# RWKV scan on TensorE: readout and update in one tiling mode, a block-diagonal inverse, alternating heads in the Gram, and two runs moved into others

## The chip, the cores and the metric

The kernel runs on one core of one Trainium2 chip. The metric is the device time of one execution in microseconds (us), lower is better. The engines are TensorE (PE in the profile; its weight loads are PEld), VectorE (DVE), ScalarE (ACT), GpSimd (POOL) and SyncE (SP), which issues nearly all DMAs. Each engine works through its own instructions in order.

## The reference, cut to what matters

One layer with two groups of heads: 16 heads of forgetting attention ("fox", head dimension 128) and 32 RWKV-7 heads (dimension 64), behind one wide input projection and ahead of one output projection. Everything is float32; the sequence has 256 frames, the model 4096 columns.

```
proj = x @ w_in                      # fox q|k|v|f, rwkv r|k|v|w_down|a_down, gate z
...
state = state * w_t + (state @ a_t) b_t^T + v_t k_t^T     # per head, per frame
y_t   = state @ r_t
...
out = concat(fox, rwkv) * silu(z) @ w_out
x   = LayerNorm(ALPHA * x + out)
```

The kernel computes the recurrence of `state` in chunks of 64 frames: within a chunk the frames are coupled by a strictly triangular 64x64 matrix per head, whose inverse (with the unit diagonal) has to be applied once per chunk, and the state is carried from chunk to chunk.

## The kernel before, in words

**The main stream.** The work goes in 16 groups `i`; a group is two RWKV heads (64 rows each, so together the 128 partitions) and one fox head. For each group eight projections of 128 columns are computed (r, k, v, fox q, k, v, and two gates). Float32 weights and inputs are split into a high and a low fp32r part. `proj` (L198) loads a weight tile of 128x1024 by DMA on SyncE (L204, four buffers), ScalarE makes its high part (L135), VectorE its low part by a subtraction (L136; three buffers each), and `mm` (L139) issues for each of 32 k-blocks a pair of matmuls: the high part against 512 columns (L140) and the low part against 256 (L141). A projection is four such tiles of eight pairs.

**Slots.** After every fourth pair `slot()` (L191) advances each of a list of Python generators by one `yield`, and what they emit falls between two pairs of the main stream in TensorE's order. So a group has 64 slots, two per weight tile: one at the tile's end and one at its middle. `wait(n)` lets n slots pass; the waits of the stages are in the table `W` (L38). The framework then places tiles in buffers, adds the waits, and orders the instructions of each engine; an instruction of another engine can come earlier than its place in the code when its inputs are there. (The product of bonus and v, L451, stands after the inverse in the code and runs beside the Gram.)

**`rwkv(i)` (L364), in order:**

1. Inputs: k, the normalisation, `lt[j]` and `BK`, which hold the decayed left and right factors of the two heads `j`; `HALF[j]` are the rows of head `j`.
2. The Gram run (L406): 4 chunks for head 0, then 4 chunks for head 1, each a product of 64 rows with 128 stationary and 128 streamed columns into the PSUM tile `gp[j]`. VectorE masks one half of the result into `gb` (L415) and the other into the free half of `lt[j]` (L424). Right behind it four transposes of BK (L427).
3. The triangular blocks of 32x32 go through DRAM into another layout: `nd` (L419), `Nb` (L421). VectorE computes the inverse of all blocks row by row (L438, L439), and the result returns through `td` (L443) and four loads `T` (L446).
4. A run of v against the centring matrix (`vp`, L457), copied by ScalarE to the upper or lower halves of `SV[j]` and `UV[j]` (L462, L463).
5. `X`: four transposes of T on VectorE (L469), then two runs of 32x32 products, `qt` (L474) and `xp` (L484), that fill the off-diagonal blocks; the result of xp is copied into X for head 0 by ScalarE and for head 1 by VectorE (L487).
6. The scan over the 4 chunks c, a slot after each step: the residual `rh` (L494) and its copy R (L496); the update `up`, X times R for each head (L501), copied into `UV` (L502, L503); the new state `sp` (L508; not in the last chunk) and, in the same run, the readout `yp`: for each head one product of SV with lt (L521, 128 rows) and one of UV with gb (L522, the head's 64 rows).
7. Group norm and the gate (L525 to L543).

`fox(i)` (L545) loads `nb` (the cumulated gate of the keys, L548), and computes logits, softmax (L565 to L569), transposes of the probabilities (L573, copied to `pT`, L574) and the output (L578, copied to `o`, L580).

**Tilings.** A matmul uses the 128x128 array as a whole or a part of its rows and columns. The profile prints rows*columns of the stationary operand: 128*128 for the main stream, 64*128 for the Gram, 128*64 for rh, sp and L521, 64*64 for vp, up and L522, 32*32 for qt and xp. A float32 product appears as two matmul instructions, so the Gram of a group is x16 and rh of a chunk x4.

## Time and profile before

| | us |
|---|---|
| three runs | 2138.33, 2138.70, 2142.48 (median 2138.7) |
| the profiled execution, first to last instruction (span) | 2139.2 |
| the same less the median of the runs | 0.5 |
| TensorE busy, share of the span | 98% |
| VectorE, ScalarE | 69%, 48% |
| input projections and scan, from 70 to 1759 us: TensorE, VectorE, ScalarE busy | 1668.9, 1211.4, 827.9 of 1689.0 |
| TensorE clock granted, mean | 0.994 |

The page of the profile gives no other time of the profiled execution than its span. Rows of the timeline have the start, the duration, the engine, the line, the operation, the tiles written and read, the shape and how many instructions of the kind follow each other (x4). Matmuls are pipelined and their durations overlap, so starts say more than durations. In rows of groups the number before the comma is the busy time in all, then the mean in ns, then the idle time of the engine before such instructions and what ended it. In rows of waits the numbers are the total, the times and the longest. In rows of windows each engine has its busy time and, in brackets, the matmuls or loads in flight.

### The profile page before, as it was taken

Reading aid. Unit: us, or ns where it says so; the run is one execution under the profiler, and the core shown is the slowest. Engines: PE = TensorE matmul, PEld = TensorE weight load, DVE = VectorE, ACT = ScalarE, POOL = GpSimd, SP = SyncE. Lnnn points to the kernel's source line nnn. Section 1 sums busy time; section 2 is a strip of 40 time slices with the busy share of each in tenths; the row PEclk is TensorE's granted clock in tenths of the full one; section 3 lists DMA queues with packets and bytes.
Section 4 is the critical chain, followed back from the end, with each engine's and each line's share of the span. In section 5 each row is a group of like instructions: output and inputs, shape, how many; then the busy total and the mean of one; then the engine's idle time right before and its main releaser. Section 6 shows DMA issues by size and latency. Waiting matters only on the chain.

```text
span 2139.2 us, 33113 instructions
## 1 busy us (share of the span) xinstructions
PE 2103.2 (98%) x12558; PEld 1745.4 (82%) x12558; DVE 1478.6 (69%) x2919; ACT 1020.9 (48%) x1607; POOL 29.4 (1%) x136
## 2 busy tenths in 40 slices
PE   9999999999999999999999999999999999999997
PEld 7878887878888888887888888888888877888885
DVE  6867676767676777776676767676767686655555
ACT  6545454545454545454545454444444454433332
POOL 0000000000000000000000000000000000000000
PEclk9999999999999999999999999999999999999998
DMA  7545555545555555555555555555555555866664
GB/s 279 183 145 174 161 172 160 167 162 161 171 163 166 167 165 167 168 164 169 156 172 159 175 159 176 159 172 162 167 162 169 154 175 188 276 196 190 194 195 150
DMA packets 130865, 372.73 MB, mean 174 GB/s; under 512 B 31161, under 2 KB 40041, under 8 KB 130705
## 3 DMA queue, kind: packets, MB, share of 16 engines
q1 hardware_dynamic: 130704, 370.62, 55.3%
q8 instruction: 98, 1.61, 0.3%
q14 instruction: 63, 0.51, 0.1%
HBM read 364.23 MB, written 6.32 MB: 173 GB/s over the span
## 4 chain that ended last, share of the span: by engine, by line
PE 75%; DVE 16%; DMA 6%; issue 2%; ACT 1%; SPq 1%; DVEq 0%; ACTq 0%
PE acc L140 33%; PE acc L141 16%; PE oacc L661 6%; PE oacc L663 5%; PE oacc L662 5%; DVE xc L439 3%; DVE prod L438 3%; DVE w_1l L136 2%; DMA td<-xc 2%; DVE w_2l L136 2%; PE yp L522 2%; DMA T<-td 1%; DVE w_0l L136 1%; DMA w<-in_w_main_dram 1%; PE gp L406 1%
## 5 line engine op out<-in xcount | busy, mean ns | idle before, releaser
L140 PE MATMUL acc<-x,w_1h 128*128 128x512 f32 x1016 | 374.9, 406 | 0.4 <-ACT w_1h L135 0.4
L140 PE MATMUL acc<-x,w_2h 128*128 128x512 f32 x1016 | 374.8, 405 | 0.0
L140 PE MATMUL acc<-x,w_3h 128*128 128x512 f32 x1016 | 374.3, 405 | 0.0
L140 PE MATMUL acc<-x,w_0h 128*128 128x512 f32 x1016 | 371.3, 404 | 0.0
L141 PE MATMUL acc<-x,w_1l 128*128 128x256 f32 x1016 | 288.7, 284 | 14.2 <-DVE w_1l L136 14.2
L141 PE MATMUL acc<-x,w_2l 128*128 128x256 f32 x1016 | 285.5, 281 | 0.0
L141 PE MATMUL acc<-x,w_3l 128*128 128x256 f32 x1016 | 284.9, 280 | 0.0
L141 PE MATMUL acc<-x,w_0l 128*128 128x256 f32 x1016 | 284.9, 280 | 0.0
L140 PEld LDWEIGHTS acc<-x,w_3h 128*128 128x128 f32 x1016 | 190.6, 188 | 47.8
L140 PEld LDWEIGHTS acc<-x,w_0h 128*128 128x128 f32 x1016 | 190.7, 188 | 47.5
L140 PEld LDWEIGHTS acc<-x,w_1h 128*128 128x128 f32 x1016 | 191.5, 189 | 46.2 <-ACT w_1h L135 0.7
L140 PEld LDWEIGHTS acc<-x,w_2h 128*128 128x128 f32 x1016 | 191.2, 188 | 43.4
L135 ACT CAST w_2h<-w 128x1024 fp32r<-128x1024 f32 x127 | 133.3, 1050 | 179.4 <-PE acc L140 117.7
L141 PEld LDWEIGHTS acc<-x,w_1l 128*128 128x128 f32 x1016 | 192.6, 190 | 23.1 <-DVE w_1l L136 23.0
L135 ACT CAST w_1h<-w 128x1024 fp32r<-128x1024 f32 x127 | 132.9, 1046 | 151.6 <-PE acc L140 150.1
L135 ACT CAST w_0h<-w 128x1024 fp32r<-128x1024 f32 x127 | 133.1, 1048 | 138.4 <-PE acc L140 102.9
L136 DVE TENSOR_TENSOR w_1l<-w,w_1h 128x1024 fp32r<-128x1024 f32 x127 | 154.3, 1215 | 62.6 <-ACT w_1h L135 62.1
L141 PEld LDWEIGHTS acc<-x,w_2l 128*128 128x128 f32 x1016 | 192.5, 189 | 0.7
L141 PEld LDWEIGHTS acc<-x,w_3l 128*128 128x128 f32 x1016 | 192.0, 189 | 0.7
L141 PEld LDWEIGHTS acc<-x,w_0l 128*128 128x128 f32 x1016 | 191.9, 189 | 0.1
L136 DVE TENSOR_TENSOR w_0l<-w,w_0h 128x1024 fp32r<-128x1024 f32 x127 | 155.0, 1220 | 47.0 <-ACT w_0h L135 45.3
L136 DVE TENSOR_TENSOR w_2l<-w,w_2h 128x1024 fp32r<-128x1024 f32 x127 | 155.2, 1222 | 39.2 <-ACT w_2h L135 39.2
(690 smaller groups left out, 3305.0 us busy)
## 6 DMA issues: line engine op xcount, KB each, us to landing
w<-in_w_main_dram SPq DMA_DIRECT2D x508, 512.0 KB, 4.6
wo<-in_w_o_dram SPq DMA_DIRECT2D x128, 512.0 KB, 3.4
Nb<-nd SPq DMA_DIRECT2D x16, 512.0 KB, 6.4
res<-in_xtok_dram SPq DMA_DIRECT2D x16, 256.0 KB, 5.0
xr<-in_xt_dram SPq DMA_DIRECT2D x7, 512.0 KB
out_dram<-res SPq DMA_DIRECT2D x7, 512.0 KB, 2.7
lr<-in_w_lora_dram SPq DMA_DIRECT2D x7, 416.0 KB, 8.4
nb<-ncd SPq DMA_DIRECT2D x16, 128.0 KB, 4.4
```

What stands on the lines that cost most here:

```text
L135: nc.scalar.copy(hi[:, :n], src[:, :n])
L136: nc.vector.tensor_tensor(lo[:, :n], src[:, :n], hi[:, :n].bitcast(F32), ALU.subtract)
L140: nc.tensor.matmul(acc[:m, :], hi[:, o : o + m], xs[k].rearrange("p a t -> p (a t)"), start=(k == 0), stop=False)
L141: nc.tensor.matmul(acc[:m, :S], lo[:, o : o + m], xs[k][:, 0, :], start=False, stop=(k == KT - 1))
L406: nc.tensor.matmul(gp[j][:, c * P : (c + 1) * P], BK[h, c, :], lt[j][h, c, :], start=True, stop=True)
L438: nc.vector.tensor_tensor(prod[:, :, s + 1 :], nb[:, s : s + 1, s + 1 :].to_broadcast([P, NJ, w]), xc[:, :, s + 1 :], ALU.mult)
L439: nc.vector.tensor_reduce(xc[:, :, s : s + 1], prod[:, :, s:], AX.X, ALU.add)
L522: nc.tensor.matmul(dst, UV[j][h, c, :], gb[h, c, C:P], start=False, stop=True)
L661: nc.tensor.matmul(acc[m], ht[k][:, 0, tt], hi[:, o], start=(k == 0), stop=False)
L662: nc.tensor.matmul(acc[m], ht[k][:, 1, tt], hi[:, o], start=False, stop=False)
L663: nc.tensor.matmul(acc[m], ht[k][:, 0, tt], lo[:, o], start=False, stop=(k == KT - 1))
```

## The change

- The readout's second product takes all 128 rows: `gb` becomes two tiles that live through the whole kernel, `gb[0]` and `gb[1]`, each zero in the rows of the other head, zeroed once by GpSimd. Now sp and both readout products have the tiling 128*64. They are issued SV for head 0, SV for head 1, UV for head 0, UV for head 1.
- `X` becomes a tile of 128 columns with the two heads' inverses on its diagonal, and the update is one product of 128x128 with R instead of one per head.
- The Gram issues chunk by chunk, head 0 and head 1 in turn.
- The run `vp` moves from behind the inverse to directly behind the Gram, ahead of the transposes of BK, and takes 128 rows (`cent` is block-diagonal) instead of 64. Its copies and the product of bonus and v move with it.
- The residual of the first chunk moves into the run of `xp`; the slot between the two goes, so that the scan's later steps each come one slot sooner.
- `pT` uses the buffer of `nb`, and `o` that of `vt`.

```diff
@@ -176,8 +176,11 @@
     nc.vector.memset(gneps, GN_EPS)
     onesr = const.tile([P, P], F32R, name="onesr")
     nc.vector.tensor_copy(onesr, ones)
-    X = const.tile([P, NCH, C], F32, name="X")
+    X = const.tile([P, NCH, P], F32, name="X")
     nc.gpsimd.memset(X, 0.0)
+    gb = [const.tile([P, NCH, P], F32, name=f"gb{j}") for j in range(2)]
+    for j in range(2):
+        nc.gpsimd.memset(gb[j], 0.0)
 
     sides = []
 
@@ -400,11 +403,19 @@
         done.add(i)
         yield from wait(W["gp"])
         gp = [pst(f"gp{i}_{j}") for j in range(2)]
-        for j in range(2):
-            h = HALF[j]
-            for c in range(NCH):
+        for c in range(NCH):
+            for j in range(2):
+                h = HALF[j]
                 nc.tensor.matmul(gp[j][:, c * P : (c + 1) * P], BK[h, c, :], lt[j][h, c, :], start=True, stop=True)
-        gb = rp.tile([P, NCH, P], F32, tag="gb", name=f"gb{i}")
+        v = rk[i, 2]
+        vp = pst(f"vp{i}")
+        for c in range(NCH):
+            for j in range(2):
+                h, o = HALF[j], HALF[1 - j]
+                nc.tensor.matmul(vp[o, c * C : (c + 1) * C], v[:, c * C : (c + 1) * C], cent[:, h], start=True, stop=True)
+        tp = pst(f"tp{i}")
+        for c in range(NCH):
+            nc.tensor.transpose(tp[:, c * P : (c + 1) * P], BK[:, c, :], ident)
 
         def m(rows):
             return cs[rows, C_MASK : C_MASK + P].unsqueeze(1).to_broadcast([C, NCH, P])
@@ -412,21 +423,27 @@
         gv = [gp[j].rearrange("p (c t) -> p c t", t=P) for j in range(2)]
         for j in range(2):
             h = HALF[j]
-            nc.vector.tensor_tensor(gb[h], gv[j][h], m(h), ALU.mult)
+            nc.vector.tensor_tensor(gb[j][h], gv[j][h], m(h), ALU.mult)
...
-            nc.sync.dma_start(out=nd[q].rearrange("c r s -> r c s"), in_=gb[B * q : B * (q + 1), :, o : o + B])
+            nc.sync.dma_start(out=nd[q].rearrange("c r s -> r c s"), in_=gb[q // 2][B * q : B * (q + 1), :, o : o + B])
         nb = rp.tile([P, B, B], F32, tag="Nb", name=f"Nb{i}")
         nc.sync.dma_start(out=flat(nb), in_=nd.rearrange("q c r s -> (q c) (r s)").unsqueeze(1).to_broadcast([16, NG, B * B]))
         for j in range(2):
             o = HALF[1 - j]
             nc.vector.tensor_tensor(lt[j][o], gv[j][o], m(o), ALU.mult)
-        tp = pst(f"tp{i}")
-        for c in range(NCH):
-            nc.tensor.transpose(tp[:, c * P : (c + 1) * P], BK[:, c, :], ident)
         BKt = rp.tile([P, NCH, P], F32, tag="sbl", name=f"BKt{i}")
         nc.scalar.copy(flat(BKt), tp)
+        SV = [rp.tile([P, NCH, C], F32, tag=f"SV{j}", name=f"SV{j}_{i}") for j in range(2)]
+        UV = [rp.tile([P, NCH, C], F32, tag=f"UV{j}", name=f"UV{j}_{i}") for j in range(2)]
+        for j in range(2):
+            o = HALF[1 - j]
+            nc.scalar.copy(SV[j][o], ch(vp[:, :S])[o])
+            nc.scalar.copy(UV[j][o], ch(vp[:, :S])[o])
+            nc.gpsimd.memset(SV[j][HALF[j], 0, :], 0.0)
+        nc.vector.tensor_tensor(bon, bon, v, ALU.mult)
+        nc.scalar.activation(bon, bon, AF.Identity, bias=column("gn_bias", i))
         yield from wait(W["d1"])
         prod = rp.tile([P, NJ, B], F32, tag="prod", name=f"prod{i}")
         xc = rp.tile([P, NJ, B], F32, tag="xc", name=f"xc{i}")
@@ -444,61 +461,48 @@
         T = rp.tile([P, NCH, B], F32, tag="T", name=f"T{i}")
         for q in range(4):
             nc.sync.dma_start(out=T[B * q : B * (q + 1)], in_=td[q].rearrange("c r s -> r c s"))
-        yield from wait(4)
-        while (i, 2) not in rk:
-            yield
-        v = rk[i, 2]
-        nc.vector.tensor_tensor(bon, bon, v, ALU.mult)
-        nc.scalar.activation(bon, bon, AF.Identity, bias=column("gn_bias", i))
-        vp = pst(f"vp{i}")
-        for c in range(NCH):
-            for j in range(2):
-                h, o = HALF[j], HALF[1 - j]
-                nc.tensor.matmul(vp[o, c * C : (c + 1) * C], v[h, c * C : (c + 1) * C], cent[h, h], start=True, stop=True)
-        SV = [rp.tile([P, NCH, C], F32, tag=f"SV{j}", name=f"SV{j}_{i}") for j in range(2)]
-        UV = [rp.tile([P, NCH, C], F32, tag=f"UV{j}", name=f"UV{j}_{i}") for j in range(2)]
-        for j in range(2):
-            o = HALF[1 - j]
-            nc.scalar.copy(SV[j][o], ch(vp[:, :S])[o])
-            nc.scalar.copy(UV[j][o], ch(vp[:, :S])[o])
-            nc.gpsimd.memset(SV[j][HALF[j], 0, :], 0.0)
-        yield from wait(W["d2"] - 4)
+        yield from wait(W["d2"])
         for q in range(4):
-            o = B * (q % 2)
+            o = C * (q // 2) + B * (q % 2)
             rows = slice(B * q, B * (q + 1))
             nc.vector.transpose(X[rows, :, o : o + B], T[rows])
         qp = pst(f"qt{i}")
         for c in range(NCH):
             for j in range(2):
                 a, b = slice(C * j, C * j + B), slice(C * j + B, C * j + C)
-                nc.tensor.matmul(qp[b, c * B : (c + 1) * B], gb[a, c, B:C], T[a, c, :], start=True, stop=True)
+                nc.tensor.matmul(qp[b, c * B : (c + 1) * B], gb[j][a, c, B:C], T[a, c, :], start=True, stop=True)
         Q = rp.tile([P, NCH, B], F32, tag="Q", name=f"Q{i}")
         for j in range(2):
             b = slice(C * j + B, C * j + C)
             (nc.vector.tensor_copy if j else nc.scalar.copy)(flat(Q)[b], qp[b, :P])
+
+        def residual(c):
+            rh = pst(f"rh{i}_{c}")
+            for j in range(2):
+                nc.tensor.matmul(rh[HALF[j], :C], lt[j][:, c, 0:C], SV[j][:, c, :], start=True, stop=True)
+            R = rp.tile([P, C], F32, tag="R", name=f"R{i}_{c}", bufs=2)
+            nc.vector.tensor_copy(R, rh[:, :C])
+            return R
+
         yield from wait(W["xp"])
         xp = pst(f"xp{i}")
         for c in range(NCH):
             for j in range(2):
                 a, b = slice(C * j, C * j + B), slice(C * j + B, C * j + C)
-                nc.tensor.matmul(xp[a, c * B : (c + 1) * B], Q[b, c, :], X[b, c, B:], start=True, stop=True)
+                nc.tensor.matmul(xp[a, c * B : (c + 1) * B], Q[b, c, :], X[b, c, C * j + B : C * j + C], start=True, stop=True)
         for j in range(2):
             a = slice(C * j, C * j + B)
-            (nc.vector.tensor_copy if j else nc.scalar.copy)(X[a, :, B:], xp[a, :P].rearrange("p (c s) -> p c s", s=B))
+            (nc.vector.tensor_copy if j else nc.scalar.copy)(X[a, :, C * j + B : C * j + C], xp[a, :P].rearrange("p (c s) -> p c s", s=B))
+        R = residual(0)
         yield
 
         yp = pst(f"yp{i}")
         for c in range(NCH):
-            rh = pst(f"rh{i}_{c}")
-            for j in range(2):
-                nc.tensor.matmul(rh[HALF[j], :C], lt[j][:, c, 0:C], SV[j][:, c, :], start=True, stop=True)
-            R = rp.tile([P, C], F32, tag="R", name=f"R{i}_{c}", bufs=2)
-            nc.vector.tensor_copy(R, rh[:, :C])
-            yield
+            if c:
+                R = residual(c)
+                yield
             upp = pst(f"up{i}_{c}")
-            for j in range(2):
-                h = HALF[j]
-                nc.tensor.matmul(upp[h, :C], X[h, c, :], R[h, :], start=True, stop=True)
+            nc.tensor.matmul(upp[:, :C], X[:, c, :], R, start=True, stop=True)
             nc.vector.tensor_copy(UV[0][HALF[0], c, :], upp[HALF[0], :C])
             nc.scalar.copy(UV[1][HALF[1], c, :], upp[HALF[1], :C])
             yield
@@ -515,11 +519,9 @@
                         sl_ = rp.tile([P, C], F32, tag=f"sl{j}", name=f"sl{i}_{c}_{j}")
                         nc.scalar.mul(sl_[h], SV[j][h, c, :], lc)
                         nc.vector.scalar_tensor_tensor(SV[j][h, c + 1, :], sp[h, :C], lc, sl_[h], ALU.mult, ALU.add)
-            for j in range(2):
-                h = HALF[j]
-                dst = yp[h, c * C : (c + 1) * C]
-                nc.tensor.matmul(dst, SV[j][:, c, :], lt[j][:, c, C:P], start=True, stop=False)
-                nc.tensor.matmul(dst, UV[j][h, c, :], gb[h, c, C:P], start=False, stop=True)
+            for lhs, rhs in ((SV, lt), (UV, gb)):
+                for j in range(2):
+                    nc.tensor.matmul(yp[HALF[j], c * C : (c + 1) * C], lhs[j][:, c, :], rhs[j][:, c, C:P], start=lhs is SV, stop=lhs is UV)
             yield
 
         y2 = rt(f"y2{i}")
@@ -571,13 +573,13 @@
         pt = pst(f"fpt{i}")
         for m in range(3):
             nc.tensor.transpose(pt[:, m * P : (m + 1) * P], lg[:, m, :], ident)
-        pT = rp.tile([P, 3 * P], F32, tag="pT", name=f"pT{i}")
+        pT = rp.tile([P, 3 * P], F32, tag="nb", name=f"pT{i}")
         nc.scalar.copy(pT, pt[:, : 3 * P])
         yield from wait(W["fo"])
         op = pst(f"fop{i}")
         nc.tensor.matmul(op[:, :S], vt[:, 0, :], pT[:, :S], start=True, stop=False)
         nc.tensor.matmul(op[:, P:S], vt[:, 1, :], pT[:, S:], start=False, stop=True)
-        o = t256("fo", f"fo{i}")
+        o = t256("vt", f"fo{i}")
         nc.scalar.copy(o, op[:, :S])
         while f"f{i}" not in szs:
             yield
```

## The prediction

> **What bounds the kernel now.** I read the totals and the chain of waits first, then the matmuls of one scan in order of time, then the waits.
>
> ```profile
> PE 2103.2 (98%) x12558; PEld 1745.4 (82%) x12558; DVE 1478.6 (69%) x2919; ACT 1020.9 (48%) x1607; POOL 29.4 (1%) x136
> ...
> PE 75%; DVE 16%; DMA 6%; issue 2%; ACT 1%; SPq 1%; DVEq 0%; ACTq 0%
> ...
> L141 PE MATMUL acc<-x,w_1l 128*128 128x256 f32 x1016 | 288.7, 284 | 14.2 <-DVE w_1l L136 14.2
> ```
>
> TensorE is busy 98% of the span and is three quarters of the chain; the clearest wait inside its main stream is 14.2 us for the low halves of the weights. So time is gained by taking work or dead time out of TensorE's order, as long as VectorE and the DMAs behind it don't turn the gain into a wait. The change touches the small products that interrupt the stream of pairs L140, L141. The timeline of TensorE gives what one interruption costs:
>
> ```profile
> 1000.92 0.28 PE L141 MATMUL acc<-x,w_3l 128*128 128x256 f32 x1
> 1001.13 0.34 PE L494 MATMUL rh<-SV,lt 128*64 128x64 f32 x4
> ...
> 1001.73 0.28 PE L141 MATMUL acc<-x,w_3l 128*128 128x256 f32 x1
> 1001.85 0.40 PE L140 MATMUL acc<-x,w_3h 128*128 128x512 f32 x1
> 1002.08 0.28 PE L141 MATMUL acc<-x,w_3l 128*128 128x256 f32 x1
> ...
> 1002.80 0.28 PE L141 MATMUL acc<-x,w_3l 128*128 128x256 f32 x1
> 1003.00 0.33 PE L501 MATMUL up<-R,X 64*64 64x64 f32 x4
> ...
> 1003.60 0.28 PE L141 MATMUL acc<-x,w_0l 128*128 128x256 f32 x1
> ...
> 1004.66 0.28 PE L141 MATMUL acc<-x,w_0l 128*128 128x256 f32 x1
> 1004.87 0.34 PE L508 MATMUL sp<-UV,BKt 128*64 128x64 f32 x4
> 1005.03 0.28 PE L521 MATMUL yp<-lt,SV 128*64 128x64 f32 x2
> 1005.24 0.33 PE L522 MATMUL yp<-gb,UV 64*64 64x64 f32 x2
> 1005.50 0.33 PE L521 MATMUL yp<-lt,SV 128*64 128x64 f32 x2
> 1005.76 0.32 PE L522 MATMUL yp<-gb,UV 64*64 64x64 f32 x2
> ...
> 1006.35 0.28 PE L141 MATMUL acc<-x,w_0l 128*128 128x256 f32 x1
> ```
>
> Durations overlap, so I count from start to start. An undisturbed pair takes 0.355 (1001.73 to 1002.08, and 0.36 for 1002.08 to 1002.80 halved). A run costs the time from the L141 before it to the first L141 behind it, less 0.355: rh 0.81 - 0.355 = 0.455, up 0.80 - 0.355 = 0.445, state update with readout 1.69 - 0.355 = 1.335. Each f32 product counts twice (x4 is two products), which I call passes.
>
> ```profile
> 984.36 0.28 PE L141 MATMUL acc<-x,w_3l 128*128 128x256 f32 x1
> 984.57 0.68 PE L457 MATMUL vp<-cs,s 64*64 64x64 f32 x16
> ...
> 985.51 0.28 PE L141 MATMUL acc<-x,w_3l 128*128 128x256 f32 x1
> ...
> 998.94 0.28 PE L141 MATMUL acc<-x,w_2l 128*128 128x256 f32 x1
> 999.15 0.44 PE L484 MATMUL xp<-X,Q 32*32 32x32 f32 x16
> ...
> 999.86 0.28 PE L141 MATMUL acc<-x,w_3l 128*128 128x256 f32 x1
> ```
>
> vp is busy 0.68 for 16 passes where rh is busy 0.34 for 4, so a further pass adds (0.68 - 0.34) / 12 = 0.028 when the two halves alternate. Of rh's 0.455 that leaves 0.34 for going into a tiling and out of it: 0.17 a switch. vp costs 0.80, xp 0.565.
>
> **The change part by part**, per group of 16.
>
> *Readout and state update in one tiling.* The second readout product becomes 128 rows deep, so all 12 passes stand in the tiling 128x64 and the heads alternate. Cost: 0.34 + 12 x 0.028 = 0.68 instead of 1.335; three internal switches go, and pairs of passes run side by side. The last chunk has no state update: 0.34 + 8 x 0.028 = 0.56, against 1.335 - 0.11 = 1.22. Saved: 3 x 0.655 + 0.66 = 2.62. The added zeros cost no columns. Bounds: if the readout passes don't pair, each takes some 0.055 (half of what a pass of 128 columns takes in the Gram below, 0.107) and the run 1.0, saving 0.33 a chunk.
>
> *Update through the block-diagonal inverse.* Two passes of a full 128x128 product take the place of four in tiles: no switch remains. No row has 128 stationary columns with only 64 streamed. The nearest is the slot of L141 (1001.73 to 1001.85), 0.12 with the next 128 columns loaded beneath it; a pass here streams a quarter of the columns at the f32 cost, and I take the load as its limit: 0.11 each, 0.22 the pair. Saved 0.445 - 0.22 = 0.225 a chunk, 0.90 a group. Bounds: 0.11 the pair (streaming alone) to 0.445 (no gain).
>
> *First residual in xp's run.* One switch fewer: 0.17 saved. But it also takes a slot, four pairs or 1.42 us, from between xp and the first update, and the update needs X, which two copies write from xp:
>
> ```profile
> 1000.26 1.22 DVE L136 TENSOR_TENSOR w_1l<-w,w_1h 128x1024 fp32r<-128x1024 f32 x1 [1.57 <-ACT w_1h L135]
> 1001.52 0.29 DVE L487 COPY X<-xp 32x128 f32<-32x128 f32 x1
> 1001.84 0.23 DVE L496 COPY R<-rh 128x64 f32<-128x64 f32 x1
> ...
> 1008.03 0.23 DVE L496 COPY R<-rh 128x64 f32<-128x64 f32 x1 [1.43 <-PE rh L494]
> 1008.73 1.23 DVE L136 TENSOR_TENSOR w_3l<-w,w_3h 128x1024 fp32r<-128x1024 f32 x1 [0.48 <-ACT w_3h L135]
> ```
>
> The second X copy stands behind a subtraction of weights on VectorE and ends at 1001.81, 2.66 after xp's start (999.15). The first update now comes 0.71 (xp's start to L141) + 0.29 (residual and its switch) + 3 x 0.355 + 0.12 = 2.18 after xp's start. So TensorE will wait about 0.5 there in every group, with the whole stream queued behind the update. Bounds: 0, if the copy comes ahead of the subtraction as R does at 1008.03; 0.8, if R too comes behind X. I take 0.55.
>
> *Gram alternates heads, v's product and the transposes in one run.*
>
> ```profile
> 942.19 0.28 PE L141 MATMUL acc<-x,w_1l 128*128 128x256 f32 x1
> 942.40 1.71 PE L406 MATMUL gp<-lt,BK 64*128 64x128 f32 x16
> 944.04 0.66 PE L427 MATMUL tp<-cs,BK 128*128 128x128 f32 x4
> ...
> 944.77 0.28 PE L141 MATMUL acc<-x,w_2l 128*128 128x256 f32 x1
> ...
> 942.80:942.81 0.01, 0.01 (x2) 0.01 (x2) 1.00 0.00 0
> 943.20:943.21 0.01, 0.01 (x5) 0.01 (x4) 1.00 0.00 0
> ```
>
> The last two rows are windows of 10 ns on L406 alone: 2 matmuls in flight while only the first head's are at hand, 5 once the second head's have come into reach. So row tiles already run side by side in the middle of this run, and half of the 16 passes go alone. The run lasts 1.71 / 16 = 0.107 a pass counted singly; pairing the eight that go alone saves 4 x 0.107 = 0.43. The run costs 2.58 - 0.355 = 2.225 now, and then 2.225 - 0.43 + 16 x 0.028 (vp) + 0.17 (one more switch inside) = 2.41, against 2.225 + 0.80 apart: 0.61 saved on TensorE, or 0.18 if the heads don't pair. The run now needs v, and then frees the inverse's inputs:
>
> ```profile
> 941.84 0.48 DVE L240 SCALAR_TENSOR_TENSOR s<-s_8p,prm,s_8d 128x256 f32<-128x256 f32 x1
> ...
> 944.31 0.69 DVE L424 TENSOR_TENSOR lt<-gp,cs 64x512 f32<-64x512 f32 x1
> 944.93 0.69 DVE L415 TENSOR_TENSOR gb<-gp,cs 64x512 f32<-64x512 f32 x1
> ...
> DVE X L469 <- DMA T<-td: 46.4, 21, 3.9
> ...
> DVE prod L438 <- DMA Nb<-nd: 34.6, 16, 3.5
> ```
>
> v ends at 942.32, before the Gram starts at 942.40. What is late next is the inverse: VectorE waits for Nb in all 16 groups (2.2 us each) and for T (2.9 a group); the weights' low halves queue behind those waits in VectorE's order, and TensorE waits for them in turn. TensorE would reach that place 0.61 earlier. But the inverse starts earlier too: the second head's gb mask (944.93) now stands behind lt's (944.31); with both heads' Gram done together it can go ahead by that mask's 0.69, and the nd writes, Nb, T and X with it. So the 0.61 stays. Bounds: 0 if the masks keep their order, 0.61.
>
> *Placed at nothing:* pT in nb's buffer makes the next group's nb load on SyncE wait for this group's last attention product, and the weight loads issued behind it on SyncE with it; nb itself is read a whole group later, and the weights have four buffers, so only a wait of several tiles would reach TensorE. o in vt's buffer waits for a product that it reads anyway. The four copies of vp move to behind the Gram on ScalarE, which is 48% busy; without that room they would delay a weight cast. The zeroing of the two gb tiles and the larger X comes once, on a GpSimd that is 1% busy.
>
> *Sum per group:* 2.62 + 0.90 + 0.17 + 0.61 - 0.55 = 3.75, times 16 = 60. The profiled span is 2139.2, half a microsecond above the median of the runs (2138.7), so 2139 - 60 = 2079.
>
> **A rule against it.** By the Trainium skill, TensorE: Matmul & The Clock Gate, Part 3, a weight load overlaps a matmul in flight only when the row group differs. Full-depth products share all row groups, so by this the loads of the full update would stand open (rival 4 gives its time). This trace disagrees: the two loads of a pair use the same row groups, PEld is busy 82% under a PE busy 98%, and a pair's 0.355 has no room for open loads.
>
> **The rivals.**
> 1. *No wait at the first update* (R and X copies ahead of the subtraction). For: R at 1008.03. Against: X at 1001.52. The sum is 4.30 a group: 2139 - 69 = 2070.
> 2. *The Gram's part is lost*: the masks keep their order, or the heads don't pair, and the inverse's wait takes back 0.61 a group. For: VectorE's waits for T and Nb. 2079 + 10 = 2089.
> 3. *The readout passes don't pair* because each adds into the place of the one before. The run is then 0.34 + 12 x 0.055 = 1.0 (0.78 in the last chunk), a loss of 3 x 0.32 + 0.22 = 1.2 a group: 2098. Against: the two passes of one product already add into one place.
> 4. *The update's loads stand open*: each pass 0.11 for its load and 0.055 for streaming, the pair 0.33 instead of 0.22, 0.11 x 64 = 7 us: 2086.
> 5. *Slower*: the scan moves by one slot, half a weight tile, so its VectorE copies meet the weight subtraction at another place. If VectorE runs the subtraction (done at 1001.48, 2.54 after the tile's boundary at 998.94) ahead of them, the first and third update and the second and fourth residual wait 0.8 to 0.9 each: 3.5 a group, 56 us, 2126, still a gain. Slower needs over 4.3 a group: where two subtractions go ahead in two of the four places, it is 3.5 + 2 x 1.22 = 5.9, or 95 against the 69 gained, and 2165. Against: R at 1008.03 ran before w_3l, and one such queue is all that the rows show.
> 6. *It does not do what it says*, the tilings still alternating: about 2139.
>
> **How the numbers follow.** Forecast 45%, rival 1 20%, rival 2 17%, rival 3 8%, rival 4 4%, rival 5 4%, rival 6 2%. The range goes from 2063 (rival 1 with the update's pair at 0.11, its lower bound, in all chunks: 0.11 x 64 = 7 us) to 2099 (rival 3, rounded) and leaves out rivals 5 and 6. 0.2% is 4.3 us, about the spread of the three runs (2138.33 to 2142.48). Faster 0.94, same 0.03, slower 0.03.
>
> **What would show it.** Right: L508 with both readout lines as one unbroken block costing 0.68; the update 0.22 without a longer L140 behind it; one block Gram, vp, tp of 2.4; TensorE idle some 0.5 before each group's first update, released by X on VectorE; waits for T about as now. Wrong: passes 0.055 apart in the readout; a wait at the first update of zero or above 1; waits for w_1l well above 14 us; any new wait in the main stream.

## The result and the profile after

| | before | after |
|---|---|---|
| median of 4 runs, us | 2139.44 (2138.33 to 2142.48) | 2079.57 (2072.34 to 2084.24) |
| ratio | | 0.9713, 95% interval 0.9686 to 0.9741 |
| profiled execution (span), us | 2139.2 | 2077.5 |

The forecast was 2079. The three rows of the page that the prediction opened with now read:

```profile
PE 2030.4 (98%) x12430; PEld 1711.2 (82%) x12430; DVE 1482.1 (71%) x2919; ACT 1017.7 (49%) x1607; POOL 25.0 (1%) x138
...
PE 71%; DVE 17%; DMA 8%; issue 2%; SPq 1%; ACT 1%; DVEq 0%; ACTq 0%
...
L141 PE MATMUL acc<-x,w_1l 128*128 128x256 f32 x1016 | 289.2, 285 | 23.5 <-DVE w_1l L136 23.5
```

TensorE's part of the chain fell from 75% to 71%, the DMAs' rose from 6% to 8%, and the wait for the low half `w_1l` from 14.2 us to 23.5. So TensorE lost work, and something off TensorE took part of the gain. The timeline of TensorE in the scan, for one full chunk's update with readout and, behind it, the next chunk's update (columns: start, duration, engine, line, operation, shapes, count):

```profile
969.78 0.28 PE L141 MATMUL acc<-x,w_3l 128*128 128x256 f32 x1
969.99 0.34 PE L512 MATMUL sp<-UV,BKt 128*64 128x64 f32 x4
970.16 0.29 PE L524 MATMUL yp<-lt,SV 128*64 128x64 f32 x4
970.27 0.29 PE L524 MATMUL yp<-gb,UV 128*64 128x64 f32 x4
...
970.82 0.28 PE L141 MATMUL acc<-x,w_0l 128*128 128x256 f32 x1
...
973.74 0.29 PE L141 MATMUL acc<-x,w_0l 128*128 128x256 f32 x1
973.86 0.33 PE L505 MATMUL up<-R,X 128*128 128x64 f32 x2
...
974.31 0.28 PE L141 MATMUL acc<-x,w_1l 128*128 128x256 f32 x1
```

By the prediction's count (from the L141 before a run to the first L141 behind it, less 0.355) the state update with readout costs 1.04 - 0.355 = 0.685 instead of 1.335, the update 0.57 - 0.355 = 0.215 instead of 0.445. The Gram, v's product and the transposes stand in one block:

```profile
909.02 0.28 PE L141 MATMUL acc<-x,w_1l 128*128 128x256 f32 x1
909.23 1.16 PE L409 MATMUL gp<-lt,BK 64*128 64x128 f32 x16
910.32 0.69 PE L415 MATMUL vp<-cs,s 128*64 128x64 f32 x16
910.94 0.66 PE L418 MATMUL tp<-cs,BK 128*128 128x128 f32 x4
...
911.67 0.28 PE L141 MATMUL acc<-x,w_2l 128*128 128x256 f32 x1
```

The block costs 2.65 - 0.355 = 2.295, where the Gram with its transposes and v's product cost 2.225 + 0.80 = 3.025 apart. The same count over every run that stands in the projections' stream, with the means that the text below uses (a gap is time beyond the undisturbed spacing between two matmuls of the main stream where no run stands):

| run on TensorE | before | after | us in all, before to after |
|---|---|---|---|
| state update and readout; in the last chunk readout alone | 1.331; 1.219 | 0.690; 0.576 | 78.2 to 39.7 |
| update | 0.450 | 0.242 (median 0.217) | 27.0 to 14.8 |
| xp and the four residuals of a group | 0.564 and 0.455 | 0.826 (xp and first residual), 0.452 | 36.7 to 33.5 |
| Gram, transposes, v's product | 3.022 | 2.308 | 48.4 to 36.9 |
| softmax's transposes (fpt) | 1.162 | 1.629 | 18.6 to 26.1 |
| gaps in the main stream | | | 14.2 to 21.0 |

The four runs that the change touches gave 190.3 - 124.9 = 65.4 us (some chunks of the last group fall behind the projections and are not in it). The two last rows took 7.5 + 6.8 = 14.3 back. A pair of the main stream went from 0.3520 to 0.3500 on average over some 3700 undisturbed pairs, 7 us more gained that no term of the prediction has. 65.4 - 14.3 + 7 = 58; the last projection pair starts 56.7 earlier (1701.8 instead of 1758.5), and 5 more come behind it, which makes the 61.7 of the spans. A second profiled execution of the changed kernel (experiment 5, 5 us shorter) has the four runs within 0.01 us of these means, but 29.2 in the softmax's run and 14.3 in the gaps. So the two last rows, and they alone, vary by some us from one execution to the next.

**The first update does not wait, but in the last group.** TensorE from xp to the first update, and VectorE beside it:

```profile
965.94 0.28 PE L141 MATMUL acc<-x,w_2l 128*128 128x256 f32 x1
966.15 0.44 PE L492 MATMUL xp<-X,Q 32*32 32x32 f32 x16
966.52 0.34 PE L482 MATMUL rh<-SV,lt 128*64 128x64 f32 x4
...
968.86 0.28 PE L141 MATMUL acc<-x,w_3l 128*128 128x256 f32 x1
968.98 0.33 PE L505 MATMUL up<-R,X 128*128 128x64 f32 x2
```
```profile
967.26 1.23 DVE L136 TENSOR_TENSOR w_1l<-w,w_1h 128x1024 fp32r<-128x1024 f32 x1
968.52 0.29 DVE L495 COPY X<-xp 32x128 f32<-32x128 f32 x1
```

The copy of X stands behind a weight subtraction and ends at 968.81, 2.66 after xp's start: exactly the time that the prediction read in the trace of before. But the update comes 2.83 after xp's start, not 2.18: between the residual and the update stand six pairs of the main stream, not four, in 15 of the 16 groups. The framework let two pairs of the next slot pass the update, so the wait has work in it. In the last group four pairs stand there, and the update waits 1.0 for the copy of X.

**The masks come later, and the wait moves to the softmax.** VectorE behind the Gram of 909.23:

```profile
910.35 1.22 DVE L136 TENSOR_TENSOR w_0l<-w,w_0h 128x1024 fp32r<-128x1024 f32 x1 [0.75 <-ACT w_0h L135]
911.49 1.40 DVE L426 TENSOR_TENSOR gb<-gp,cs 64x512 f32<-64x512 f32 x2
912.81 1.38 DVE L435 TENSOR_TENSOR lt<-gp,cs 64x512 f32<-64x512 f32 x2
```

Both masks of `gb` do stand together, ahead of those of `lt`, as foreseen. But a weight subtraction now stands ahead of them, which stood behind all masks in the trace of before:

```profile
946.25 1.21 DVE L136 TENSOR_TENSOR w_0l<-w,w_0h 128x1024 fp32r<-128x1024 f32 x1
```

`gb` is done 3.66 after the Gram's start, in the trace of before 3.22. So the inverse starts no earlier (its first product on Nb comes 12.8 after the Gram's start in the median, before 12.7), and TensorE arrives at what hangs on it 0.7 earlier. The waits for it on VectorE, to be set beside the prediction's two rows, and the place where TensorE meets them:

```profile
DVE X L468 <- DMA T<-td: 41.4, 16, 4.4
...
DVE prod L455 <- DMA Nb<-nd: 40.4, 16, 3.9
```
```profile
955.74 0.63 DVE L468 STREAM_TRANSPOSE X<-T 32x128 f32<-32x128 f32 x2 [2.58 <-DMA T<-td]
...
957.33 0.35 DVE L571 TENSOR_SCALAR lg<-lg,fst 128x256 f32<-128x256 f32 x1
957.71 0.31 DVE L468 STREAM_TRANSPOSE X<-T 32x128 f32<-32x128 f32 x1
958.05 1.23 DVE L136 TENSOR_TENSOR w_1l<-w,w_1h 128x1024 fp32r<-128x1024 f32 x1
```
```profile
957.30 0.28 PE L141 MATMUL acc<-x,w_0l 128*128 128x256 f32 x1
957.42 0.76 PE L575 MATMUL fpt<-cs,lg 128*128 128x128 f32 x3
...
959.33 0.39 PE L141 MATMUL acc<-x,w_1l 128*128 128x256 f32 x1 [0.92 <-DVE w_1l L136]
```

The first of these fences is from the waits (total, times, longest), the second VectorE's timeline, the third TensorE's. Two transposes of T stand on VectorE ahead of the softmax's last steps and wait 2.58 for T's DMA. The softmax (L571) and the subtraction of `w_1l` queue behind them; TensorE's fpt and the first L141 behind it wait for these. The run costs 2.03 - 0.355 = 1.675 there, where 0.33 would do.

### The profile page after: what moved, and what is told of

Its sections match the earlier page's. It is cut to its first block, busy times and chain, and to the rows that moved or that the text cites. A ratio compares the mean times of both kernels' runs of the same rounds, so it can differ in the third digit from the quotient of the medians.

```text
span 2077.5 us, 32862 instructions
## 1 busy us (share of the span) xinstructions
PE 2030.4 (98%) x12430; PEld 1711.2 (82%) x12430; DVE 1482.1 (71%) x2919; ACT 1017.7 (49%) x1607; POOL 25.0 (1%) x138
## 4 chain that ended last, share of the span: by engine, by line
PE 71%; DVE 17%; DMA 8%; issue 2%; SPq 1%; ACT 1%; DVEq 0%; ACTq 0%
PE acc L140 31%; PE acc L141 15%; PE oacc L663 6%; PE oacc L664 6%; PE oacc L665 6%; DVE xc L456 4%; DVE prod L455 3%; DVE w_1l L136 3%; DMA td<-xc 2%; DMA Nb<-nd 2%; DMA T<-td 2%; DMA nd<-gb 2%; DVE w_2l L136 2%; DVE w_3l L136 1%; DVE w_0l L136 1%
## 5 line engine op out<-in xcount | busy, mean ns | idle before, releaser
L140 PE MATMUL acc<-x,w_3h 128*128 128x512 f32 x1016 | 369.1, 401 | 0.0
L141 PE MATMUL acc<-x,w_1l 128*128 128x256 f32 x1016 | 289.2, 285 | 23.5 <-DVE w_1l L136 23.5
L141 PE MATMUL acc<-x,w_2l 128*128 128x256 f32 x1016 | 284.9, 280 | 0.0
L141 PE MATMUL acc<-x,w_0l 128*128 128x256 f32 x1016 | 284.6, 280 | 0.0
L141 PE MATMUL acc<-x,w_3l 128*128 128x256 f32 x1016 | 284.3, 280 | 0.0
L141 PEld LDWEIGHTS acc<-x,w_1l 128*128 128x128 f32 x1016 | 192.9, 190 | 33.6 <-DVE w_1l L136 33.6
L141 PEld LDWEIGHTS acc<-x,w_2l 128*128 128x128 f32 x1016 | 192.3, 189 | 0.9 <-DVE w_2l L136 0.2
L141 PEld LDWEIGHTS acc<-x,w_3l 128*128 128x128 f32 x1016 | 191.8, 189 | 1.0 <-DVE w_3l L136 0.3
L141 PEld LDWEIGHTS acc<-x,w_0l 128*128 128x128 f32 x1016 | 191.9, 189 | 0.5 <-DVE w_0l L136 0.3
```

The costliest lines, as they stand in the source:

```text
L140: nc.tensor.matmul(acc[:m, :], hi[:, o : o + m], xs[k].rearrange("p a t -> p (a t)"), start=(k == 0), stop=False)
L141: nc.tensor.matmul(acc[:m, :S], lo[:, o : o + m], xs[k][:, 0, :], start=False, stop=(k == KT - 1))
```

## The experiments

The theory from these profiles: TensorE's runs give what was computed, some 70 us, and 10 us or more of it are lost because VectorE runs its queue in an order in which a transpose waiting for T from DRAM holds up the softmax and the weights. The rivals: the loss is a cover that v's product used to give at its old place; or the parts themselves are worth less than their rows. Ratios are to the kernel before, run beside it on the same chip.

**1. The readout alone.** The kernel before, with `gb` as two tiles, the readout in one tiling, and the shared buffers of `pT` and `o`.

```diff
-            for j in range(2):
...
-                nc.tensor.matmul(dst, UV[j][h, c, :], gb[h, c, C:P], start=False, stop=True)
+            for lhs, rhs in ((SV, lt), (UV, gb)):
+                for j in range(2):
+                    nc.tensor.matmul(yp[HALF[j], c * C : (c + 1) * C], lhs[j][:, c, :], rhs[j][:, c, C:P], start=lhs is SV, stop=lhs is UV)
```

> The kernel before with the readout's change alone (two zero-padded gb tiles, state update and readout in one tiling; the buffers of pT and o shared to make room). Theory (TensorE's runs give what their passes and switches cost, and nothing behind them takes it back in the scan): the run falls from 1.33 to 0.69 us, 0.65 x 64 chunks = 41 us, so about 2098. Rival (the readout passes do not pair, rival 3 of the prediction): run 1.0, 20 us, so about 2119. Rival (the gain needs the other parts, because a wait on VectorE is late next in the scan): well under 41, with TensorE waiting at residual or update.

Measured: 2093.57, ratio 0.9797 [0.9778, 0.9816], 43.7 us less than before on that chip (2137.24; by the interval 39 to 47). The part is worth what its rows say: the run costs 0.684 in its trace.

**2. The update alone.** The kernel before, with the block-diagonal X and one full product.

```diff
-            for j in range(2):
-                h = HALF[j]
-                nc.tensor.matmul(upp[h, :C], X[h, c, :], R[h, :], start=True, stop=True)
+            nc.tensor.matmul(upp[:, :C], X[:, c, :], R, start=True, stop=True)
```

> The kernel before with the block-diagonal update alone (pT and o in shared buffers as in the change). Theory (two loads of 128 columns hidden under the passes, two switches gone): the run falls from 0.45 to 0.22 us, 0.23 x 64 = 15 us, so about 2124. Rival (loads stand open): 0.33, 7 us, so about 2132.

Measured: 2125.68, ratio 0.994 [0.9919, 0.9961], 11.6 us less. The interval is 9 us wide, so this agrees with the 14.4 computed and does not sharpen it. The row decides better: in its trace the update costs 0.218, not the rival's 0.33.

**3. The Gram and v's product undone.** The changed kernel with the Gram's old order and v's product behind the inverse in its old tiling.

```diff
-        for c in range(NCH):
-            for j in range(2):
-                h = HALF[j]
+        for j in range(2):
+            h = HALF[j]
+            for c in range(NCH):
...
-        yield from wait(W["d2"])
+        yield from wait(4)
+        v = rk[i, 2]
...
+                nc.tensor.matmul(vp[o, c * C : (c + 1) * C], v[h, c * C : (c + 1) * C], cent[h, h], start=True, stop=True)
...
+        yield from wait(W["d2"] - 4)
```

> The changed kernel with the Gram's head order and the place and tiling of v's product put back. TensorE's runs then cost 3.02 instead of 2.29 us a group, 12 us in all. Theory (the inverse's way through DRAM is what is late there, so that time saved ahead of it turns into waiting): only a third or so of it shows, 2082 to 2085, and the wait at the probabilities' transposes falls from about 1.3 to about 0.8 us a group. Rival (the 12 us are all gained in the changed kernel): about 2092, with the same waits as the changed kernel.

Measured: 2073.23, ratio 0.9696 [0.9675, 0.9716]. Both expectations missed: with TensorE's runs there 12 us dearer, the kernel is no slower than the changed one (0.973 [0.9708, 0.9752] in experiment 5). The softmax's run costs 14.0 in all instead of 26.1 or 29.2 (the two profiles of the changed kernel) and the gaps 14.7 instead of 21.0 or 14.3. So this part of the change gained nothing: the wait at the softmax took it all back.

**4. The update held at its place.** The changed kernel, in which the pairs of the next slot may not pass the first update in TensorE's order.

```diff
+        with tc.issue_after(queue[0]) if queue else nullcontext():
+            nc.tensor.matmul(acc[:m, :], hi[:, o : o + m], xs[k].rearrange("p a t -> p (a t)"), start=(k == 0), stop=False)
...
+            if c == 0:
+                queue.extend([ins.ins] * 16)
```

> The changed kernel with the first update held at its place in the code: the main stream's pairs behind it may no longer be issued ahead of it (in the changed kernel six pairs, not four, stand between the first residual and the first update). Theory (the copy of X ends late, and the framework hid that by moving two pairs ahead): TensorE waits 0.5 to 0.6 us before each first update, 8 to 10 us, so about 2088. Rival (the copy would have been in time, and the two pairs were moved for nothing): no wait, about 2080.

Measured: 2094.2, ratio 0.9791 [0.9774, 0.9809], 14 us slower than the change. Its timeline of TensorE at the first update:

```profile
979.17 0.28 PE L144 MATMUL acc<-x,w_3l 128*128 128x256 f32 x1
979.86 0.43 PE L509 MATMUL up<-R,X 128*128 128x64 f32 x2 [0.42 <-DVE X L499]
```

The wait that the prediction computed is there as soon as the pairs stay behind the update: it stands 0.57 behind its place (0.69 instead of the 0.12 of 973.74 to 973.86), released by the copy of X. On average the update costs 0.405 instead of 0.242 over 61 chunks, 9.9 us, as the theory had it. The time is 6 us above the 2088 expected: in this trace the softmax's run costs 30.8 instead of 26.1, near the 29.2 of the changed kernel's second profile.

**5. The changed kernel again,** unchanged, beside the next three on one chip.

> The changed kernel unaltered, on the same chip as the three runs beside it: 2079, as a base for differences of a few microseconds.

Measured: 2080.32 (2074.06 to 2085.36), ratio 0.973 [0.9708, 0.9752].

**6. v's product alone put back.** As 3, but the Gram keeps the alternating heads.

> The changed kernel with v's product alone put back behind the inverse (64 rows); the Gram still alternates, and VectorE still has a weight subtraction ahead of the masks. TensorE's runs cost 0.17 us a group more, 3 us. Theory A (v's product, 0.80 us, was cover for the wait on T): the wait at the probabilities' transposes falls by most of 0.8 and the time to about 2073, as with both parts undone. Theory B (the masks that now come 0.45 us later are what costs): no better than the changed kernel, 2079 to 2082.

Measured: 2055.22, ratio 0.9613 [0.9592, 0.9633]. Both expectations missed by 18 us and more on the fast side. The timeline of VectorE at the place of the wait says why:

```profile
942.44 0.35 DVE L572 TENSOR_SCALAR lg<-lg,fst 128x256 f32<-128x256 f32 x1
943.17 1.23 DVE L136 TENSOR_TENSOR w_1l<-w,w_1h 128x1024 fp32r<-128x1024 f32 x1 [0.38 <-ACT w_1h L135]
944.32 1.29 DVE L469 STREAM_TRANSPOSE X<-T 32x128 f32<-32x128 f32 x4
```

The framework has put the four transposes behind the softmax and behind `w_1l`; when VectorE reaches them T is there. The softmax's run costs 0.33 in the median (10.5 in all), the gaps 2.8 in all. The gaps have a place of their own. VectorE at its wait for Nb, in the changed kernel and, below, in this one:

```profile
923.62 0.17 DVE L455 TENSOR_TENSOR prod<-Nb,xc 128x4 f32<-128x4 f32 x1 [3.87 <-DMA Nb<-nd]
...
925.16 1.22 DVE L136 TENSOR_TENSOR w_3l<-w,w_3h 128x1024 fp32r<-128x1024 f32 x1
```
```profile
909.03 1.23 DVE L136 TENSOR_TENSOR w_3l<-w,w_3h 128x1024 fp32r<-128x1024 f32 x1 [1.21 <-ACT w_3h L135]
...
911.55 0.17 DVE L440 TENSOR_TENSOR prod<-Nb,xc 128x4 f32<-128x4 f32 x1 [1.29 <-DMA Nb<-nd]
```

Here the subtraction of `w_3l` stands ahead of the wait for Nb, in 15 of the 16 groups; in the changed kernel, and in the kernel before, it stands behind it. Between 15 and 30 us after the Gram's start, where TensorE waits for the low halves of the weights, the gaps are 0.8 in all instead of 16.4 (11.9 in the second profile). TensorE's runs still pay for v's product apart (in the median Gram and transposes 1.674, v's product 0.805, together 0.19 a group above the changed kernel's 2.287), so it isn't TensorE's own work that made this faster. What v's product moved was VectorE's order.

**7. The masks first.** The changed kernel, with the one weight subtraction queued behind the masks.

```diff
+        with tc.issue_after(masks[2]) if len(masks) == 3 else nullcontext():
+            nc.vector.tensor_tensor(lo[:, :n], src[:, :n], hi[:, :n].bitcast(F32), ALU.subtract)
```

> The changed kernel with the one weight subtraction that stands ahead of the gb masks on VectorE queued behind them. The masks end about 1.1 us sooner after the Gram's start (2.5 instead of 3.66). Theory B (masks late): the whole inverse comes up to 1.1 us sooner, the wait at the probabilities' transposes falls, up to 15 us gained, 2064 to 2070. Theory A (cover) with the DRAM trip bound by the transfers around it: the loads of nd and Nb land when they did, 2077 to 2080.

Measured: 2067.71, ratio 0.967 [0.9653, 0.9687], 12 us less than the change. VectorE behind a Gram that starts at 902.60:

```profile
903.79 1.41 DVE L433 TENSOR_TENSOR gb<-gp,cs 64x512 f32<-64x512 f32 x2 [0.83 <-PE gp L416]
```

The masks end 2.60 after the Gram's start, near where the prediction's argument puts them (3.22 - 0.69 = 2.53). VectorE waits 31.9 for Nb instead of 40.4 (35.9 in the changed kernel's second profile), the gaps are 11.1, and a wait of 3 us for T in the first group's run of qt, which the changed kernel has in both profiles, is gone. But masks that end 1.06 earlier bring the inverse's first product only 0.3 to 0.6 earlier on average (12.5 after the Gram's start instead of 13.1 and 12.8). The softmax's run stays dear, 28.4 in all: the gain did not come from there, and that is another wait.

**8. The transposes later.** The changed kernel, with the four transposes of T queued behind the copy of Q.

```diff
-        for q in range(4):
...
-            nc.vector.transpose(X[rows, :, o : o + B], T[rows])
...
+            qc = (nc.vector.tensor_copy if j else nc.scalar.copy)(flat(Q)[b], qp[b, :P])
+        with tc.issue_after(qc.ins):
+            for q in range(4):
...
+                nc.vector.transpose(X[rows, :, o : o + B], T[rows])
```

> The changed kernel with VectorE's four transposes of T queued behind the copy of Q, where X is needed next, instead of ahead of the softmax's last steps and of two weight subtractions. Theory (what TensorE waits for is not T but VectorE's own queue behind the wait on T): the wait at the probabilities' transposes falls from 1.3 to near 0 us a group and the stalls for the weights' low halves behind it go too, some 20 us, about 2058. Rival (T itself is late): the wait moves on to the run of qt, which reads T, and the time stays within 5 us of 2079.

Measured: 2055.32 (2052.01 to 2056.05), ratio 0.9611 [0.9597, 0.9625], 25 us less than the change. VectorE at the place:

```profile
948.16 0.35 DVE L572 TENSOR_SCALAR lg<-lg,fst 128x256 f32<-128x256 f32 x1
948.90 1.23 DVE L136 TENSOR_TENSOR w_1l<-w,w_1h 128x1024 fp32r<-128x1024 f32 x1 [0.39 <-ACT w_1h L135]
...
954.28 0.30 DVE L473 COPY Q<-qt 32x128 f32<-32x128 f32 x1
954.61 1.30 DVE L478 STREAM_TRANSPOSE X<-T 32x128 f32<-32x128 f32 x4
```

and TensorE beside it:

```profile
951.09 0.28 PE L141 MATMUL acc<-x,w_0l 128*128 128x256 f32 x1
951.21 0.49 PE L576 MATMUL fpt<-cs,lg 128*128 128x128 f32 x3
...
951.77 0.28 PE L141 MATMUL acc<-x,w_1l 128*128 128x256 f32 x1
```

The run costs 0.68 - 0.355 = 0.325, and 6.3 in all. In its page the chain has turned over, the matmul's wait for `w_1l` has more than halved:

```profile
PE 86%; DVE 7%; DMA 5%; issue 1%; SPq 1%; ACT 0%; DVEq 0%; ACTq 0%
...
L141 PE MATMUL acc<-x,w_1l 128*128 128x256 f32 x1016 | 286.6, 282 | 10.3 <-DVE w_1l L136 10.2
```

No work was removed; VectorE's share of the chain fell from 17% to 7% by the order alone. This shows the theory for the wait on T. It also shows that the loss at the softmax is not a missing cover, since v's product stands at its new place here. The gaps hardly fell (17.0 in all): they hang on the other wait, for Nb.

**9. The same order in the kernel before.** The edit of 8 in the kernel before.

> The kernel before with one edit: the four transposes of T into X are queued on VectorE behind the copy of Q, so that the wait for T no longer stands ahead of the softmax's last steps and the weight subtractions. Theory (the queue's order cost time before the change too; it is no product of the change): the run of the softmax's transposes on TensorE costs 18.6 us in the trace of before where 16 x 0.328 = 5.3 would do, so 13 go; the waits of 14.2 in the main stream go in part. 2119 to 2127, and the change measured between two kernels with this order, to 2055.3, is then 64 to 72 us, about the 70 that TensorE's runs give and more than the 59 measured. Rival (only the change made that order costly, because only it reaches the softmax's transposes ahead of X): 2133 to 2139.

Measured: 2122.21, ratio 0.9921 [0.991, 0.9933], 17 us less: the softmax's run falls from 18.6 to 5.4 in all, the gaps from 14.2 to 10.2. So the order cost time before the change too. In the trace of before, VectorE and TensorE at that place:

```profile
987.17 0.30 DVE L469 STREAM_TRANSPOSE X<-T 32x128 f32<-32x128 f32 x1 [2.72 <-DMA T<-td]
989.08 0.30 DVE L469 STREAM_TRANSPOSE X<-T 32x128 f32<-32x128 f32 x1 [1.60 <-DMA T<-td]
...
990.34 0.35 DVE L569 TENSOR_SCALAR lg<-lg,fst 128x256 f32<-128x256 f32 x1
```
```profile
989.96 0.33 PE L573 MATMUL fpt<-cs,lg 128*128 128x128 f32 x1 [0.34 <-DVE lg L569]
990.75 0.44 PE L573 MATMUL fpt<-cs,lg 128*128 128x128 f32 x2 [0.47 <-DVE lg L569]
```

Between two kernels with this order the change is worth 2122.2 - 2055.3 = 67 us, near the 70 of TensorE's runs.

**10. Both orders.** The changed kernel with the edits of 7 and 8.

> The changed kernel with both orders at once: the one weight subtraction queued behind the Gram's masks and the four transposes of T queued behind the copy of Q. Theory (two different waits: the first shortens the wait for Nb, the second takes the wait for T off the softmax): the gains of the two single edits, 12 and 25 us, mostly add: 2043 to 2050, the run of the softmax's transposes at 5 to 7 us in sum, the waits of the main stream below 11. Rival (both remove the same lateness of VectorE): 2052 to 2056, as with the later transposes alone.

Measured: 2043.36 (2042.22 to 2044.88), ratio 0.9551 [0.9538, 0.9563]: the two gains, 12 and 25, add to 37 (2080.3 to 2043.4), so they are two waits. The softmax's run costs 6.7 in all and the gaps 9.4, as expected. This is the fastest version measured.

**11. Both orders, and v's product put back.** The edits of 6, 7 and 8.

> The changed kernel with v's product put back behind the inverse in its old tiling, and with both orders of VectorE (masks ahead of the weight subtraction, transposes behind the copy of Q). If v's product matters only through what it did to VectorE's order, then with the order fixed in both, moving it into the Gram's run is worth what TensorE's rows say: 1.674 + 0.805 - 2.287 = 0.19 a group, 3 us, so this kernel comes 2 to 5 us above the one with both orders and v's product in the Gram's run: 2045 to 2054. Rival (v's product behind the inverse gives VectorE's chain a cover that is worth more than its 0.19): 2035 to 2043, below the other.

Measured: 2066.07, ratio 0.9654 [0.9642, 0.9666]. Both expectations missed, on the slow side: 23 us above experiment 10 and 11 above experiment 6. The gaps are 17.2 and the update costs 0.342 on average.

**12. v's product put back, transposes later.** The edits of 6 and 8, to tell apart which of the two orders costs it.

> The changed kernel with v's product put back behind the inverse in its old tiling, and the four transposes of T queued behind the copy of Q; the masks keep the order that the framework gives them. The kernel with v's product back lies at 2055.2, and with both orders forced at 2066.1. Theory (the masks put first are what costs the 11 us there: behind them the weight subtraction, and with it VectorE's whole queue, falls behind TensorE): the later transposes alone take some 5 us off the softmax's run, 2047 to 2054. Rival (the later transposes cost it, because X then comes late for the rest of the group): 2063 to 2068.

Measured: 2057.55, ratio 0.9632 [0.9611, 0.9653], not to be told from experiment 6 (0.9613 [0.9592, 0.9633]). The gain of 5 did not come: the softmax's run fell from 10.5 to 7.5 in all, but the update rose from 14.1 to 20.2. Six pairs pass the first update as before (in 15 of 16 groups), but the copy of X now ends 3.19 after xp's start in the median instead of 2.66, and the update waits for it. The remaining 8.5 us of experiment 11 belong to the masks put first: the gaps are 1.4 without that edit and 17.2 with it.

Why the same edit gains 12 us in one kernel and loses 8.5 in the other can be read from VectorE's order at its wait for Nb, though no run here tests it alone. In experiments 6 and 12 `w_3l` stands ahead of that wait in 15 of 16 groups, in every other version in one group at most; their gaps between 15 and 30 us after the Gram's start are 0.8 and 0.6 in all, and 8.6 to 16.4 in the twelve other traces. With the masks put first (experiment 11) the framework puts `w_3l` behind the wait again, and the gaps there are 14.4. In the changed kernel `w_3l` stands behind it with either order of the masks, so there the edit had nothing of this kind to lose. Why the framework chooses so is not known.

## Why the prediction was right, and where its steps were wrong

The time was right to 0.6 us (2079 against 2079.57), and four of the terms were right within 2 us each. Two other steps were wrong in opposite directions: a wait of 8.8 that came only in the last group, and a loss of 11 to 14 that was put at nothing. Some 7 us from a faster main stream, which no term has, close the rest. That these errors cancel is luck; the number is better than its reasons.

| term | predicted, us | measured, us |
|---|---|---|
| state update and readout in one tiling | 16 x 2.62 = 41.9 | 16 x (3 x 0.641 + 0.643) = 41.1; alone 43.7 (experiment 1) |
| update as a full product | 16 x 0.90 = 14.4 | 64 x (0.450 - 0.217) = 14.9; alone 11.6 (experiment 2) |
| first residual in xp's run | 16 x 0.17 = 2.7 | 16 x (1.019 - 0.826) = 3.1 |
| Gram and v's product, on TensorE | 16 x 0.61 = 9.8 | 16 x (3.022 - 2.308) = 11.4 |
| a wait before the first update | -16 x 0.55 = -8.8 | 61 x (0.217 - 0.242) = -1.5, nearly all in the last group |
| the inverse's chain | 0 | -14.3: softmax -7.5, gaps -6.8; in the second profile -10.7: softmax -10.6, gaps -0.1 |

- *The price of a switch (0.17) and of a further pass (0.028)* were right. In the last chunk the readout stands alone: its 8 passes cost 0.576 and rh's 4 passes cost 0.455, so a further pass costs 0.030. So the readout's passes pair although each adds into the place of the one before, and rival 3, with 0.055 a pass and a run of 0.78, is refuted. The 4 passes of the state update add 0.690 - 0.576 = 0.114, 0.0285 each.
- *The update's load as its limit, 0.22*: 0.217. Rival 4 is refuted with it. By the Trainium skill, TensorE: Matmul & The Clock Gate, Part 3, a weight load runs beside a matmul only if it goes to another row group; both loads here go to all rows, and by rival 4's estimate the pair would have cost 0.33. The measured 0.217 decides against it for these products. (The same Part of that page of the Trainium skill also lets a load run ahead when it targets the background weight buffer, which the 0.217 does not contradict.)
- *"So TensorE will wait about 0.5 there in every group"* failed. VectorE's side was exact (X done 2.66 after xp's start, in the median of both traces). What failed was TensorE's side: the prediction took the program's slots for TensorE's order, and the framework put six pairs before the update instead of four. Experiment 4 gives the step its due: with the pairs held, the wait comes, 0.57 in the group shown, and so it does in the last group of the changed kernel, where four pairs stand.
- *"So the 0.61 stays"* failed. The argument was that the masks would end 0.69 earlier and the inverse with them. The masks could have: experiment 7 has them at 2.60. But VectorE took a weight subtraction first, so they ended at 3.66. And the inverse follows its masks only in part: experiment 7 brings the masks 1.06 earlier and its first product only 0.3 to 0.6 earlier. TensorE, now 0.7 earlier, met the softmax and the weights that wait behind the transposes of T. This is rival 2 by its effect and its mechanism (the inverse's wait takes the gain back), only in another place than "the masks keep their order": their order among themselves did change. Experiment 3 shows that the part gained nothing.
- *What was next late* was named rightly (T and Nb), but only its growth was asked after. In the rows of before, the wait for T already stood ahead of the softmax, at a cost of 18.6 for a run that needs 16 x 0.33 = 5.3; experiment 9 took 17 us from the kernel before by that alone.
- Of what the prediction named as signs, the unbroken readout block, the update's price and the one block (2.3 instead of 2.4) came, and the wait for T stayed about as it was (41.4 after 46.4). The idle 0.5 before each first update did not come, and the wait for `w_1l` rose from 14.2 to 23.5; the prediction had named both as signs of being wrong.

## What to carry to other kernels

Where a framework orders an engine's instructions, a step that waits for a DMA holds up all that stands behind it in that queue, and an edit elsewhere can move it: read in the trace what stands behind the waiting instruction, and pin the order before judging the edit. Work taken out of TensorE's stream is worth its rows only when the queues that feed it are not made to wait; here the TensorE terms were right within 2 us each, and two edits to the order of one VectorE queue were worth 37 us, nearly as much as the readout. A pin that helps one version can hurt another, so it is measured again after each change.

## What the runs showed that was not expected

- An undisturbed pair of the main stream takes 0.350 us on average in the changed kernel and in experiments 4, 5, 7, 8 and 10, against 0.3507 to 0.3525 in the kernel before and wherever v's product stands apart (experiments 1 to 3, 6, 9, 11, 12). Over 3700 pairs 0.002 are 7 us. Its cause stays open.
- The alternating heads in the Gram gained more than computed: the Gram with its transposes fell from 2.222 to 1.674 in the median (experiment 6), 0.55 instead of 0.43.
- The spread of the runs changed with the order of a queue: 12 us between the lowest and highest run of the changed kernel (2072.34 to 2084.24), 3 to 4 us in experiments 8 and 10. That the arrival of T sets the first is argued, not shown.
